# A hybrid diffusion backbone on one core: the MLP of both layers in two phases with seven products of the output kind, x kept in place

## The chip, the cores and the metric

One core of a Trainium2 chip runs the whole program in one launch. The metric is the device time in microseconds (us), the median over runs; the profile is one further execution, recorded by the hardware.

## The reference, cut to what matters

Two layers work on 1024 latent tokens of width 1024, and on 256 context tokens that only layer 0 carries on. Layer 0 mixes tokens by a Fourier part beside a state-space part, layer 1 by differential attention. Each layer then has the MLP that the change rewrites: hidden width 4096, squared ReLU, and a gated residual whose gate comes from the conditioning.

```python
def sq_relu_mlp(h, w1, w2):
    return jnp.square(jax.nn.relu(h @ w1)) @ w2
...
        x = x + g2 * sq_relu_mlp(modulate(rmsnorm(x, norm2_g[i]), sh2, sc2), mlp_w1[i], mlp_w2[i])
        if not last:
...
            ctx = ctx + cg2 * sq_relu_mlp(modulate(rmsnorm(ctx, norm2_g[i]), csh2, csc2), mlp_w1[i], mlp_w2[i])
```

## The kernel before, in words

Everything is kept feature by token: x of the latent tokens is a tile xL of 8 x 1024 columns on 128 partitions, x of the context is xC of 8 x 256. Latent tokens go in two blocks, t0 = 0 and t0 = 512, of 512 columns each; the context is a third block of 256. Every operand of a product is split into a high and a low part (`split`: a cast on ACT gives the high part, a subtraction on POOL or DVE the low one), and `mm3` (L341 to L343) makes three matmuls of a product.

The order of the work is written out by hand: a line of the program puts an instruction at the end of its engine's queue, and each engine takes its queue in order. Side work comes from generators in `bg`: `self.step()` at chosen places of the MLP emits the next small piece of the first one. These are the norm of the next stage (`norm`, L436: `norm_scale` with the matmuls L392 and L406, then `norm_apply` per 128 features) and `ada_dve` (L516 on), which makes the modulation of layer 1 on DVE out of 48 loads of 512 KB, with four or eight instructions of 256 columns for each load and column of the conditioning, and small matmuls L526. The class with `load`, `split`, `get` and `done` (L136 to L200) streams the weights: SP loads a raw tile into the ring R (three slots, shared with the ada loads), ACT and POOL split it into the ring W.

Layer 0 calls `mlp` (L1449 to L1506). It goes over pairs of 128 hidden features: the up products of both (banks 0 and 1, ReLU at L1465, square at L1466, split), then the down products of the pair (banks 2 to 5), which `stt` adds into x. Tile H (three buffers) holds the hidden features.

Layer 1 calls `mlp_w` (L1562 to L1738) in two phases. Phase 1 makes all hidden features; for each u (256 hidden features) DVE sums the four quarters (`results`), the seven operands are split and stored to DRAM h_w by SP (L1590). Phase 2 takes seven products for each c (512 hidden features, 0 to 6) and q (half of the output), with operands fetched by POOL's queue (L1652) into 24 tile slots and the weight sums of `down_weights` (L1517). The products rotate over 8 banks; all are summed in M apart from x, which was saved to DRAM and is fetched again; `together` (L1686) combines them on POOL, and the last four blocks of 128 hidden features are plain products. `put` writes the output (L2282).

Queues: PE takes matmuls in the order written; SP issues weight loads, ada loads and stores of h_w; POOL makes low parts and issues the fetches.

Of the kernel before, what the change touches and what calls it, by code (L numbers as in the profile page):

```python
# [201 lines left out]
class Kern:  # L202
# [988 lines left out]
    def first(self):  # L1191
# [216 lines left out]
        self.Y, self.Ypair = self.ring("Y", 3, 512), 1  # L1408
# [27 lines left out]
    def mlp_stream(self, layer):  # L1436
        I, add = self.I, self.ws.add
        up = lambda f: add(I["w1"][layer, f].rearrange("p a b -> p (a b)"))
        down = lambda f: add(I["w2"][layer, f].rearrange("p a b -> p (a b)"))
        for f in range(3):  # L1440
            up(f)
        for i in range(0, DFF // 128, 2):
            down(i)
            down(i + 1)
            for f in (i + 3, i + 4):
                if f < DFF // 128:
                    up(f)

    def mlp(self, layer, blocks, order, H, hook, before=None):  # L1449


        nf, nt = DFF // 128, sum(n for _, n in blocks)
        hb = [b.v(2, nt) for b in H]

        def up(f, w, bl, steps=()):
            o = hb[f % 3]
            for t0, n in bl:
                ps = self.bank(0, 1)[:, :n]
                hh, hl = self.hv(t0, n)
                for k in range(8):  # L1460
                    self.mm3(ps, w[:, 0, k], w[:, 1, k], hh[:, k], hl[:, k], k == 0, k == 7)
                    if k in steps and self.bg and self.bg[0][0][0] == "norm":
                        self.step()
                e = self.E.v(n)
                self.nc.scalar.activation(out=e, in_=ps, func=AF.Relu)  # L1465
                self.nc.scalar.activation(out=e, in_=e, func=AF.Square)  # L1466
                self.split(e, o[:, 0, t0:t0 + n], o[:, 1, t0:t0 + n], elo="p")
                self.step()

        def down(f, w, last):  # L1470
            for t0, n in blocks:
                for d in range(8):
                    ps = self.bank(2, 3, 4, 5)[:, :n]
                    for i in range(2):
                        a = hb[(f + i) % 3]
                        self.mm3(ps, w[i][:, 0, d], w[i][:, 1, d], a[:, 0, t0:t0 + n], a[:, 1, t0:t0 + n],
                                 i == 0, i == 1)
                    if last and (t0, n) == blocks[-1] and d == 7:
                        self.ws.pieces = 2
                        self.ws.done(1, elo="p")  # L1480
                        self.ws.done(1, elo="v")
                        self.ws.pieces = 1
                    x = self.xv(t0, n)[:, d]
                    g = self.mod_col(layer, 5, 0 if t0 < SEQ else 1)[:, d:d + 1]
                    self.stt(x, ps, g, x, ALU.mult, ALU.add)
                    if last:
                        hook(t0, n, d)
                    if last or d % 2:
                        self.step()

        w = [self.ws.get(8, 128) for _ in range(3)]
        for t0, n in order:
            if before:
                before(t0, n)
            for f in range(3):
                up(f, w[f], [(t0, n)], (0, 3, 5, 6, 7))
                if (t0, n) == order[-1]:
                    self.ws.done()
        for i in range(0, nf, 2):
            down(i, [self.ws.get(8, 128) for _ in range(2)], i + 2 >= nf)  # L1500
            if i + 2 < nf:
                self.ws.done(2)
            for f in (i + 3, i + 4):
                if f < nf:
                    up(f, self.ws.get(8, 128), blocks)
                    self.ws.done()  # L1506

# [7 lines left out]
    WINO = ("B11", "B21", "T2", "T3", "T1", "B22", "T4")  # L1515

    def down_weights(self, layer):  # L1517


        nc, I, raw = self.nc, self.I, {}  # L1520

        def load(u, i):
            raw[u, i] = r = self.R.v(1024)
            if u < 14:
                c, q = divmod(u, 2)
                o = r.rearrange("p (h f c) -> p h f c", h=2, f=2)
                for j in range(2):
                    src = I["w2"][layer, 4 * c + 2 * j + i].rearrange("p (h q d) e -> p h q (d e)", h=2, q=2)
                    nc.sync.dma_start(out=o[:, :, j], in_=src[:, :, q])
            elif u < 16:  # L1530
                o = r.rearrange("p (h f c) -> p h f c", h=2, f=4)
                for j in range(4):
                    nc.sync.dma_start(out=o[:, :, j], in_=I["w2"][layer, 28 + j][:, 2 * u - 28 + i::4])
# [5 lines left out]
        for u in range(16):  # L1539
            load(u + 1, 0)  # L1540
            A11, A21, A12, A22 = (raw[u, i][:, 512 * j:512 * j + 512] for i in range(2) for j in range(2))
            S1 = S2 = None
            for i in range(7 if u < 14 else 4):
                if i == 2 and u < 14:
                    S1, S2 = self.E.v(512), self.E.v(512)
                    self.tt(S1, A21, A22, ALU.add)
                    self.tt(S2, S1, A11, ALU.subtract)
                if i == 3 and u < 14:
                    self.tt(A21, A11, A21, ALU.subtract)
                if i == 5:  # L1550
                    self.tt(S2, A12, S2, ALU.subtract)
                src = (A11, A12, S2, A21, S1, S2, A22)[i] if u < 14 else (A11, A21, A12, A22)[i]
# [3 lines left out]
                self.split(src, w[:, 0].rearrange("p a b -> p (a b)"), w[:, 1].rearrange("p a b -> p (a b)"), elo="p")  # L1556
                n += 1
                if i == (5 if u < 14 else 1):
                    load(u + 1, 1)
                yield w  # L1560

    def mlp_w(self, layer, v0, oS, put):  # L1562


        nc, x8 = self.nc, self.xL.v(8, SEQ)
        fb, mb = self.buf("F", 2048), self.buf("M", 3072)
        dt = self.tc.dram_tile
        xd, hd = dt([128, 8, SEQ], F32R, name="x_w"), dt([16, 7, 128, 1024], F32R, name="h_w")
        fl = lambda a: a.bitcast(F32)
        for i in range(0, 8, 2):  # L1570
            nc.sync.dma_start(out=fl(xd)[:, i:i + 2], in_=x8[:, i:i + 2])

        X, L = fb.v(4, 512), self.xL.v(4, 512)
        turn = ([6, 7, 2, 3, 4, 5] * 17)[:98] + [2, 3, 6, 7, 6, 7, 6, 7]
        gen, Wq, count = self.down_weights(layer), [], [0, -1]

        def make(k=1):

            for _ in range(k):
                if count[0] < 106 and 2 * (count[0] // 2 - 3) + 1 <= count[1]:  # L1580
                    Wq.append(next(gen))
                    count[0] += 1


        def results(u, C):
            def keep(name, src, elo="p"):
                o = x8[:, turn.pop(0)].rearrange("p (a b) -> p a b", a=2)
                self.split(src, o[:, 0].bitcast(F32R), o[:, 1].bitcast(F32R), elo=elo)
                i = self.WINO.index(name) if name in self.WINO else 2
                nc.sync.dma_start(out=fl(hd)[u, i], in_=o.rearrange("p a b -> p (a b)"))  # L1590

            keep("B11", C["11"])
            yield
            if u > 13:
                for q in ("12", "21", "22"):
                    keep("B" + q, C[q])
                    yield
# [3 lines left out]
            keep("T1", T, "v")  # L1601
            yield
            keep("B22", C["22"])
            yield
            self.tt(T, C["22"], T, ALU.subtract)
            keep("T2", T)
            yield
            self.tt(C["12"], C["22"], C["12"], ALU.subtract)
            keep("T3", C["12"])
            yield  # L1610
            keep("B21", C["21"])
            yield
            self.tt(C["21"], C["21"], T, ALU.subtract)
            keep("T4", C["21"], "v")
            yield

        C, done = [{} for _ in range(16)], []

        def up(f, w, t0, beside):
            ps, (hh, hl), u = self.bank(0, 1), self.hv(t0, 512), f // 2  # L1620
# [3 lines left out]
            i = 2 * (f % 2) + t0 // 512  # L1624
            e = ((L if t0 else X)[:, f] if u < 2 else (X if u % 2 else L)[:, i])
            C[u][f"{1 + f % 2}{1 + t0 // 512}"] = e
            nc.scalar.activation(out=e, in_=ps, func=AF.Relu)
            nc.scalar.activation(out=e, in_=e, func=AF.Square)
            if f % 2 and t0:
                done.append(results(u, C[u]))  # L1630

        def norms(k):
            if k in (0, 3, 5, 6, 7) and self.bg and self.bg[0][0][0] == "norm":
                self.step()

# [6 lines left out]
        slots = [a[:, :, i, o:o + 512] for a, o in ((oS, 512), (v0, 0), (oS, 0)) for i in range(8)]  # L1642
        tiles, order = {}, [(c, j, p) for c in range(7) for j in range(7) for p in range(2)]
        order += [("x", d) for d in (0, 4, 1, 5, 2, 6, 3, 7)] + [(7, j, p) for p in range(2) for j in (0, 1, 2, 5)]

        def fetch(n):
            for _ in range(n):
                i = len(tiles)
                if i < len(order):
                    o, tiles[o] = order[i], slots[i % len(slots)]  # L1650
                    src = xd[:, o[1]] if len(o) == 2 else hd[2 * o[0] + o[2], o[1]]
                    nc.gpsimd.dma_start(out=tiles[o], in_=src.rearrange("p (a b) -> p a b", a=2))  # L1652

        w = [self.ws.get(8, 128) for _ in range(3)]
        for t0, n in LAT:
# [738 lines left out]
```

## Time and profile before

| what | value |
|---|---|
| runs | 2924.09, 2926.7, 2927.6 us, median 2926.7 |
| the profiled execution | 2926.48 us, its span 2924.7 us |
| mean granted clock of TensorE | 0.986 |
| PE busy | 2814.2 us, 96% of the span |
| DVE, POOL, ACT busy | 64%, 47%, 37% |
| DMA | 382.90 MB, 131 GB/s on average |

The span is what lies between the first and the last instruction; the 1.8 us around it do not change with the kernel's inside. Busy shares are means over very different stages. Layer 0's MLP runs from about 505 to 1420 us, layer 0's projection into layer 1 follows, and layer 1's MLP runs from about 2170 us to the end.

### The profile page before, as it was taken

To read this page: it belongs to the slowest core of one execution; us is meant where nothing else is said; L and a number is where in the kernel's file an instruction comes from. 1 tells how busy PE (TensorE), PEld (TensorE's weight loads), DVE (VectorE), ACT (ScalarE), POOL (GpSimd) and SP (SyncE) were. 2 spreads that over 40 slices of the span, in tenths; PEclk is the share of its full clock that TensorE was granted. 3 is DMA by queue.
4 is the path that set the end of the run, shared out by engine and by line. 5 is a ranking of instruction groups with operands and counts; after the bars stand their busy time and mean duration, and the time that the engine had idled before them with its cause. 6 is when DMAs were issued, how large, how long until landed. Compare 5 with 4: busy or idle time off the path is not lost.

```text
span 2924.7 us, 39807 instructions
## 1 busy us (share of the span) xinstructions
PE 2814.2 (96%) x15018; PEld 2352.2 (80%) x15018; DVE 1879.6 (64%) x3645; ACT 1077.5 (37%) x1915; POOL 1366.7 (47%) x1072
## 2 busy tenths in 40 slices
PE   5899899999999999999999999999999999999998
PEld 2666688788888888888778788999988888878887
DVE  7789867654553553232778857999976444337666
ACT  3342343322122222223334435666643544432220
POOL 5614223433232223223433425777733565568778
PEclk9999999999999999999999999999999999999999
DMA  7255540122222222101155642323224556598883
GB/s 296 88 186 165 177 133 24 44 87 73 80 87 79 80 72 74 42 29 44 44 161 159 165 127 86 98 75 108 71 87 137 201 214 232 194 309 274 252 259 123
DMA packets 240865, 382.90 MB, mean 131 GB/s; under 512 B 12960, under 2 KB 148640, under 8 KB 239648
## 3 DMA queue, kind: packets, MB, share of 16 engines
q1 hardware_dynamic: 199024, 293.31, 30.9%
q0 software_dynamic: 41648, 87.04, 9.9%
q8 instruction: 118, 1.93, 0.3%
q14 instruction: 75, 0.61, 0.1%
HBM read 270.69 MB, written 109.61 MB: 130 GB/s over the span
## 4 chain that ended last, share of the span: by engine, by line
PE 77%; DVE 12%; POOL 4%; ACT 3%; DMA 2%; issue 2%; SPq 0%; POOLq 0%; DVEq 0%; ACTq 0%
PE bank L341 20%; PE bank L342 20%; PE bank L343 20%; PE sc L1930 4%; PE pv L1970 4%; PE tb L1961 2%; DVE T L907 2%; DVE xh L911 2%; DVE E L296 2%; DVE hl L296 1%; POOL W L337 1%; PE sc L342 1%; PE sc L343 1%; PE sc L341 1%; POOL xL L324 1%
## 5 line engine op out<-in xcount | busy, mean ns | idle before, releaser
L337 POOL TENSOR_TENSOR W<-R,W 128x1024 fp32r<-128x1024 f32 (+1 forms) x170 | 340.7, 2012 | 572.3 <-issue 290.5
L296 DVE SCALAR_TENSOR_TENSOR xL<-bank,k,xL 128x512 f32<-128x512 f32 x296 | 217.7, 747 | 340.1 <-PE bank L343 339.7
L333 ACT CAST W<-R 128x1024 fp32r<-128x1024 f32 (+2 forms) x212 | 183.7, 884 | 506.7 <-PE bank L343 438.5
L341 PE MATMUL bank<-hl,W 128*128 128x512 f32 (+1 forms) x768 | 297.6, 387 | 8.1 <-ACT hl L433 3.8
L342 PE MATMUL bank<-hl,W 128*128 128x512 f32 (+1 forms) x768 | 295.3, 384 | 9.7 <-DVE hl L296 8.2
L343 PE MATMUL bank<-hl,W 128*128 128x512 f32 (+1 forms) x768 | 292.3, 381 | 1.0 <-DVE W L337 1.0
L341 PE MATMUL bank<-H,W 128*128 128x512 f32 (+1 forms) x768 | 274.6, 358 | 3.6 <-DVE xC L296 2.8
L342 PE MATMUL bank<-H,W 128*128 128x512 f32 (+1 forms) x768 | 271.8, 354 | 0.0
L343 PE MATMUL bank<-H,W 128*128 128x512 f32 (+1 forms) x768 | 271.8, 354 | 0.0
L337 POOL TENSOR_TENSOR H<-E,H 128x512 fp32r<-128x512 f32 (+1 forms) x96 | 107.9, 1124 | 231.6 <-ACT H L333 218.6
L343 PE MATMUL bank<-oS,W 128*128 128x512 f32 x536 | 208.8, 390 | 0.6 <-POOL W L337 0.6
L1935 DVE TENSOR_REDUCE S<-sc 128x1 f32<-128x1280 f32 x128 | 184.2, 1480 | 39.0 <-PE sc L1930 39.0
L342 PE MATMUL bank<-oS,W 128*128 128x512 f32 x536 | 209.0, 390 | 0.1
L341 PE MATMUL bank<-oS,W 128*128 128x512 f32 x536 | 208.9, 390 | 0.0
L341 PEld LDWEIGHTS bank<-hl,W 128*128 128x128 f32 x768 | 145.3, 189 | 58.4 <-issue 19.2
L342 PEld LDWEIGHTS bank<-hl,W 128*128 128x128 f32 x768 | 145.6, 190 | 42.3 <-DVE hl L296 14.9
L343 PE MATMUL bank<-hb,W 128*128 128x512 f32 x432 | 169.2, 392 | 3.6 <-POOL W L337 3.6
L341 PE MATMUL bank<-hb,W 128*128 128x512 f32 x432 | 169.3, 392 | 0.0
L342 PE MATMUL bank<-hb,W 128*128 128x512 f32 x432 | 168.8, 391 | 0.0
L343 PEld LDWEIGHTS bank<-hl,W 128*128 128x128 f32 x768 | 145.5, 190 | 28.6 <-DVE W L337 1.5
L1930 PE MATMUL sc<-K,W 128*128 128x512 f32 x720 | 167.8, 369 | 0.0
L341 PEld LDWEIGHTS bank<-H,W 128*128 128x128 f32 x768 | 145.2, 189 | 25.3 <-DVE xC L296 3.9
(441 smaller groups left out, 7079.9 us busy)
## 6 DMA issues: line engine op xcount, KB each, us to landing
h_w<-xL SPq DMA_DIRECT2D x106, 512.0 KB, 3.6
R<-in_w_dram SPq DMA_DIRECT2D x96, 512.0 KB, 3.7
oS<-h_w POOLq DMA_DIRECT2D x68, 512.0 KB, 7.7
R<-in_ada_w_dram SPq DMA_DIRECT2D x52, 512.0 KB, 3.6
hb<-h_w POOLq DMA_DIRECT2D x38, 512.0 KB, 7.1
W<-q_d POOLq DMA_DIRECT2D x15, 1024.0 KB, 5.4
R<-in_w_dram SPq DMA_DIRECT2D x56, 256.0 KB, 6.3
A<-in_ada_w_dram SPq DMA_DIRECT2D x24, 512.0 KB, 4.5
```

What stands on the lines that cost most here:

```text
L296: f(**kw)
L333: nc.scalar.copy(hi, src)
L337: e.tensor_tensor(out=lo, in0=src, in1=hi.bitcast(F32), op=ALU.subtract)
L341: mm(ps, lhsT=lh, rhs=rh, start=first, stop=False)
L342: mm(ps, lhsT=lh, rhs=rl, start=False, stop=False)
L343: mm(ps, lhsT=ll, rhs=rh, start=False, stop=last)
L907: v.tensor_tensor(out=b.raw(o, [[48, 2], [1, 32]]), in0=self.CAb.raw(64 * d, [[32, 2], [1, 32]]), in1=h.raw(prev[d], [[0, 2], [1, 32]]), o ...
L911: v.tensor_reduce(out=h.raw(cur[d], [[16, 2], [1, 16]]), in_=b.raw(o, [[48, 2], [1, 16], [16, 3]]), axis=AX.X, op=ALU.add)
L1930: nc.tensor.matmul(self.SC[i][:, c0:c0 + n], lhsT=Qf[:, e, q0:q0 + 128], rhs=K[:, i, c0:c0 + n], start=e == 0, stop=e == 1)
L1935: nc.vector.tensor_reduce(out=st[:, i, 1:2], in_=self.SC[i][:, 0:1280], axis=AX.X, op=ALU.max, negate=True)
L1961: nc.tensor.transpose(ps[:, 128 * j:128 * j + 128], it["P"][0][:, 128 * (c0 + j):128 * (c0 + j) + 128], self.ident)
L1970: nc.tensor.matmul(self.PV[:, 0:128], lhsT=it["wT"][:, kt], rhs=heads[h]["v"][:, kt], start=kt == 8, stop=kt == 3)
```

## The change

One function `mlp` serves both layers and has the two phases; `mlp_w` and the DRAM copy of x are gone.

- Of the seven products of a (c, q), three (j = 1, 5, 6) feed one quarter of the output only. Their results go from the bank straight into x (`to_x`). The four shared ones (j = 0, 2, 3, 4) are summed in M, 16 half tiles, and `together` has four additions on POOL and four `to_x` in place of seven additions and four.
- Products use banks 0 to 5 (8 before in layer 1). In layer 0 the context has plain down products in banks 6 and 7; `down_weights` splits an eighth half (A21) for them.
- Layer 0 has 16 tile slots in the buffers of the normalized input (h0, h1) and four for the context in hc, which are free once the up products have read them; layer 1 has 22. The splits of `results` go through 3 places (layer 0) or 4 (layer 1; 6 before).
- `up` steps the side work by two pieces a block. `self.flush()` empties it ahead of hidden block 30.
- The last products of layer 0 go in two passes over the features: blocks 0 and context first, then block 512, with three pieces of side work each.
- Layer 0's down products for the latent tokens were 1536 matmuls of 512 columns; over 28 of the 32 hidden blocks seven of eight are left. PE's queue has 11324 rows where it had 11492, 168 fewer, all of them of 512 columns.

```diff
-    def mlp(self, layer, blocks, order, H, hook, before=None):
...
-    def mlp_w(self, layer, v0, oS, put):
...
+    def mlp(self, layer, order, slots, sc, ready, hook, before):
+        nc, blocks = self.nc, sorted(order)
+        ctx = len(order) == 3
...
+        turn = ([10, 12, 14] if ctx else [8, 10, 12, 14]) * 50
...
             if ctx:
+                keep(7, place(8 + u % 2))
+                yield
+            keep(0, C["11"])
...
         def up(f, w, t0, n, beside):
...
             nc.scalar.activation(out=e, in_=ps, func=AF.Relu)
             nc.scalar.activation(out=e, in_=e, func=AF.Square)
-            if f % 2 and t0:
+            left[f] -= 1
+            if left[2 * u] + left[2 * u + 1] == 0:
                 done.append(results(u, C[u]))
+            self.step(2)
...
+        for f in range(3, 30):
             w = self.ws.get(8, 128)
+            for t0, n in blocks:
+                up(f, w, t0, n, keeps)
             self.ws.done()
+        self.flush()
+        next(gen)
+        fetch_free(None)
+        w = [self.ws.get(8, 128) for _ in range(2)]
+        free = [None]
+        for t0, n in blocks:
+            for f in (30, 31):
+                make(count[0] < 2)
+                up(f, w[f - 30], t0, n, keeps)
+            free.append(t0)
+            if t0 != blocks[-1][0]:
+                fetch_free(*free)
+        self.ws.done(2)
         make(6)
+        fetch_ctx(0)
+        fetch_free(*free)
...
+                        if j in (1, 5, 6):
+                            to_x(ps, dh if j == 6 else dl, 512 if j == 5 else 0)
                         else:
+                            m = place(M[q][j, e])
+                            if c:
+                                self.tt(m, ps, m, ALU.add)
+                            else:
+                                self.vcopy(m, ps)
+                    if ctx and j in (0, 1, 6):
+                        for e in range(2):
+                            context(w, e, int(j > 0), int(j == 6))
+                    used()
...
+        if ctx:
+            ready(0)
+            for i, d in enumerate(self.LAST):
+                last(Wq.pop(0), d, 512, 512)
+                used()
+                hook(512, 512, d, i)
+                self.step(3)
+                if i % 2:
+                    ready(i)
...
-        self.mlp(0, ALL, MIX, [H0, H1, H2], hook, before=lambda t0, n: self.flush_norm(t0))
+        slots = [(0, h0[:, :, i]) for i in range(6)] + [(512, h1[:, :, i]) for i in range(4)] + \
+                [(0, h0[:, :, i]) for i in (6, 7)] + [(512, h1[:, :, i]) for i in range(4, 8)]
...
+        self.mlp(0, MIX, slots, sc, ready, hook, before)
```

Four places where the order of instructions matters. First SP in layer 0's up phase, over one pair of hidden blocks (L1539 stores a split operand, L544 is an ada load, L149 a weight load). Before, the same loads had no stores between them:

```order
L544 DMA R_50_5350<-in_ada_w_dram 128x4x256
L149 DMA R_51_5390<-in_w_dram 128x1024
L544 DMA R_52_5439<-in_ada_w_dram 128x4x256
L544 DMA R_53_5509<-in_ada_w_dram 128x4x256
L544 DMA R_54_5578<-in_ada_w_dram 128x4x256
```

```order
L149 DMA R_90_7127<-in_w_dram 128x1024
L1539 DMA h_w_4555<-M_4839 128x1024
L1539 DMA h_w_4555<-M_4554 128x1024
L1539 DMA h_w_4555<-M_4839 128x1024
L544 DMA R_91_7167<-in_ada_w_dram 128x4x256
L1539 DMA h_w_4555<-M_4839 128x1024
```

Three stores now stand ahead of the ada load of R_91. On DVE, in the same pair, the instructions on that load (Y from R) stand ahead of sums of hidden features (E and M):

```order
L296 TENSOR_TENSOR E_184_7156<-M_4554 128x512
L337 TENSOR_TENSOR M_4839<-E_184_7156,M_4839 128x512
L296 TENSOR_SCALAR Y_16_7166<-R_91_7167,k_110 128x256
L296 SCALAR_TENSOR_TENSOR Y_16_7166<-R_91_7167,k_110,Y_16_7166 128x256
L296 TENSOR_TENSOR E_184_7156<-M_4554,E_184_7156 128x512
L296 TENSOR_TENSOR M_4554<-M_4554 128x512
```

The sum in E_184 is an operand that ACT casts ahead of the next ReLU. Next POOL at the switch of layer 0 between the phases (hl are the buffers of the two latent blocks, hc that of the context; L1604 is a fetch):

```order
L1604 DMA hl_3675<-h_w_4555 128x2x512 x6
L1604 DMA hl_3679<-h_w_4555 128x2x512 x4
L1604 DMA hl_3675<-h_w_4555 128x2x512 x2
L1604 DMA hl_3679<-h_w_4555 128x2x512 x4
L337 TENSOR_TENSOR W_57_8255<-E_189_8059,W_57_8255 128x512
L337 TENSOR_TENSOR W_57_8255<-E_190_8060,W_57_8255 128x512
L337 TENSOR_TENSOR W_58_8261<-E_188_8058,W_58_8261 128x512
L337 TENSOR_TENSOR W_58_8261<-E_189_8059,W_58_8261 128x512
L1604 DMA hc_3828<-h_w_4555 128x2x512 x4
```

The context's fetches stand last, behind sixteen others and four splits. Last PE: at `self.flush()` ahead of hidden block 30 (hc is the context's up product of block 29), and in layer 0's projection into layer 1:

```order
L343 MATMUL bank_1_61<-hc_3828,W_53_7688 128x256
L526 MATMUL bank_7_67<-k_94,Y_21_7899 128x1 x2
L526 MATMUL bank_7_67<-k_94,Y_22_7998 128x1 x2
L526 MATMUL bank_7_67<-k_94,Y_23_8014 128x1 x2
L526 MATMUL bank_7_67<-k_94,Y_24_8030 128x1 x2
L341 MATMUL bank_0_60<-hl_3675,W_54_7782 128x512
```

```order
L343 MATMUL bank_2_62<-W_122_11473,hl_3675 128x512
L392 MATMUL bank_6_66<-k_110,Y_30_11640 128x1 x4
L406 MATMUL bank_7_67<-E_272_11694,k_94 128x512
L341 MATMUL bank_3_63<-W_120_11364,hl_3679 128x512
```

The small matmuls of four chunks of `ada_dve` come one behind the other, with no product between them; in the projection the two matmuls of the norm of block 512 (L392, L406) are neighbours, where before 18 matmuls stood between them.

## Rows read from the trace of the kernel before

**Rows 1.** The page: busy time by engine, and the chain's shares by engine.

```profile
PE 2814.2 (96%) x15018; PEld 2352.2 (80%) x15018; DVE 1879.6 (64%) x3645; ACT 1077.5 (37%) x1915; POOL 1366.7 (47%) x1072
PE 77%; DVE 12%; POOL 4%; ACT 3%; DMA 2%; issue 2%; SPq 0%; POOLq 0%; DVEq 0%; ACTq 0%
```

**Rows 2.** Windows: stretch, its length, busy time (count) of each engine, clock, DMA share, GB/s.

```profile
850.00:1000.00 150.00, 150.00 (x798) 129.78 (x798) 75.37 (x124) 35.33 (x56) 43.24 (x26) 1.00 0.26 81
2614.00:2619.00 5.00, 1.38 (x5) 0.84 (x4) 1.29 (x2) 0.00 (x0) 4.70 (x6) 0.79 1.38 385
```

**Rows 3.** Timeline of the end: start, time, engine, line, operation, [idle before <-releaser].

```profile
2911.72 0.39 PE L342 MATMUL bank<-hb,W 128*128 128x512 f32 x1
...
2915.35 0.39 PE L343 MATMUL bank<-oS,W 128*128 128x512 f32 x1
2915.39 1.71 POOL L324 TENSOR_TENSOR M<-F,M 128x512 f32<-128x512 f32 x1
...
2919.55 2.05 DVE L296 SCALAR_TENSOR_TENSOR M<-bank,k,M 128x512 f32<-128x512 f32 x3
```

**Rows 4.** Timeline of layer 1's switch between the phases.

```profile
2615.16 0.71 POOL L1652 DMA_DIRECT2D oS<-h_w  x1 [0.28 <-DMA hb<-h_w]
...
2617.12 2.49 POOL L337 TENSOR_TENSOR W<-R,W 128x512 fp32r<-128x512 f32 x2
...
2618.43 0.80 PE L343 MATMUL bank<-hb,W 128*128 128x512 f32 x1 [3.62 <-POOL W L337]
```

**Rows 5.** Timeline of PE at the start of layer 0's MLP, and at its end.

```profile
516.59 0.39 PE L341 MATMUL bank<-hc,W 128*128 128x256 f32 x1 [2.05 <-ACT E L1465]
...
1416.09 0.39 PE L341 MATMUL bank<-H,W 128*128 128x256 f32 x1 [1.33 <-DVE xC L296]
1416.31 0.28 PE L342 MATMUL bank<-H,W 128*128 128x256 f32 x1
1416.43 0.29 PE L343 MATMUL bank<-H,W 128*128 128x256 f32 x1
...
1419.57 0.76 PE L341 MATMUL bank<-W,hl 128*128 128x512 f32 x1 [2.50 <-DVE xC L296]
1420.13 0.63 PE L342 MATMUL bank<-W,hl 128*128 128x512 f32 x1
...
1425.25 0.59 PE L342 MATMUL bank<-W,hl 128*128 128x512 f32 x1
```

**Rows 6.** Timeline of the norm in layer 0's projection.

```profile
1432.05 0.94 PE L392 MATMUL bank<-k,Y 128*128 128x1 f32 x8
1438.14 0.59 ACT L409 COPY Y<-bank 128x512 f32<-128x512 f32 x1 [3.01 <-PE bank L406]
1452.58 0.75 DVE L296 SCALAR_TENSOR_TENSOR hl<-E,k,hl 128x512 fp32r<-128x512 f32 x1 [0.19 <-ACT hl L433]
```

**Rows 7.** Groups by line and shape, 560 to 1370 us: count | busy, mean ns | idle before.

```profile
L341 PE MATMUL bank<-H,W 128*128 128x512 f32 x470 | 184.4, 392 | 0.7 <-DVE xL L296 0.7
L296 DVE SCALAR_TENSOR_TENSOR xL<-bank,k,xL 128x512 f32<-128x512 f32 x236 | 173.6, 748 | 295.7 <-PE bank L343 295.6
L337 POOL TENSOR_TENSOR W<-R,W 128x1024 fp32r<-128x1024 f32 x56 | 135.5, 2431 | 321.9 <-issue 267.0 <-ACT W L333 54.9
L296 DVE SCALAR_TENSOR_TENSOR Y<-R,k,Y 128x256 f32<-128x256 f32 x218 | 123.9, 598 | 34.6 <-DMA R<-in_ada_w_dram 31.7
L337 POOL TENSOR_TENSOR H<-E,H 128x512 fp32r<-128x512 f32 x56 | 72.8, 1301 | 180.4 <-ACT H L333 180.4
```

**Rows 8.** Timeline: an ada load in layer 0's MLP, and DVE's first instructions on it.

```profile
1013.51 0.38 SPq L544 DMA_DIRECT2D R<-in_ada_w_dram  x1
1017.14 1.00 DVE L296 SCALAR_TENSOR_TENSOR Y<-R,k,Y 128x256 f32<-128x256 f32 x2 [1.72 <-DMA R<-in_ada_w_dram]
```

**Rows 9.** Timeline of POOL in the norm: one operation beside little of DVE, one beside much.

```profile
1441.27 1.30 POOL L324 TENSOR_TENSOR E<-xL,Y 128x512 f32<-128x512 f32 x1
1443.73 1.74 POOL L324 TENSOR_TENSOR E<-xL,Y 128x512 f32<-128x512 f32 x1
```

More of the change, by code (lines that the diff above doesn't have):

```diff
@@ L1433, in hv @@
         return [a[:, :, t0 - b:t0 - b + n] for a in self.hx[b]]
+    WINO = ("B11", "B21", "T2", "T3", "T1", "B22", "T4")
+    LAST = (0, 1, 4, 5, 2, 3, 6, 7)
     def mlp_stream(self, layer):
[L1437 to L1447, printed above, removed]
@@ L1449, in mlp @@
-    def mlp(self, layer, blocks, order, H, hook, before=None):
[L1452 to L1506, printed above, removed]
@@ L1515, with down_weights @@
-    WINO = ("B11", "B21", "T2", "T3", "T1", "B22", "T4")
-    def down_weights(self, layer):
+        for f in range(32):
+            self.ws.add(self.I["w1"][layer, f].rearrange("p a b -> p (a b)"))
+    def down_weights(self, layer, plain, passes):
         nc, I, raw = self.nc, self.I, {}
+        end = 14 + 2 * passes
         def load(u, i):
-            raw[u, i] = r = self.R.v(1024)
+            if u < end:
+                raw[u, i] = r = self.R.v(1024)
             if u < 14:
@@ L1646, in fetch, with get @@
+        def get(o, v):
+            tiles[o] = v
+            nc.gpsimd.dma_start(out=v, in_=hd[2 * o[0] + o[2], o[1]].rearrange("p (a b) -> p a b", a=2))
+        n_slots, fetched = len(slots), [0]
         def fetch(n):
             for _ in range(n):
[L1648 to L1652, printed above, removed]
+                i = fetched[0]
+                if i < len(tasks):
+                    get(tasks[i], slots[i % n_slots][1])
+                    fetched[0] += 1
@@ L1654, in mlp_w, with fetch_free, fetch_ctx @@
+        def fetch_free(*free):
+            while fetched[0] < n_slots and slots[fetched[0]][0] in free:
+                fetch(1)
+        def fetch_ctx(c):
+            if ctx and c < 8:
+                for p in range(2):
+                    get((c, 7, p), sc[2 * (c % 2) + p])
         w = [self.ws.get(8, 128) for _ in range(3)]
-        for t0, n in LAT:
-            self.flush_norm(t0)
+        for t0, n in order:
+            before(t0, n)
+            if (t0, n) == order[-1]:
+                mem.append(self.buf("M", 2048, side="R"))
@@ L1657, in mlp_w @@
             for f in range(3):
[L1658 to L1659 removed]
+                up(f, w[f], t0, n, norms)
+                if (t0, n) == order[-1]:
                     self.ws.done()
[L1661 removed]
+        for f in range(3, 30):
             w = self.ws.get(8, 128)
[L1663 to L1673 removed]
```

299 lines of the change are left out of this document (173 added, 126 removed).

## Prediction

> **What bounds the kernel now.** I read the page first: PE is busy 96% of the span and makes 77% of the chain that ended last [rows 1]. The kernel is a stream of matmuls with a few holes, and a change is worth what it takes out of the stream and the holes it closes, less the holes it opens. The windows show the stream: from 850 to 1000 us PE is busy the whole 150 us at full clock [rows 2]. Next comes the timeline at each hole that lies in code the change touches: the end [rows 3], layer 1's switch from up to down products [rows 4], start and end of layer 0's MLP [rows 5]. DVE, ACT and POOL have room on average [rows 1], but each takes its queue in order, so a hole comes from one late item at the head of a queue.
>
> Two prices. A 512-column matmul: the one at 2911.72 and the one at 2915.35 are 16 steps apart [rows 3], 0.2269 us each (the 0.39 us in a row is the latency of one, not the pace). And what a hole costs beyond its length: after the gap of 2.50 us before 1419.57, the 12 steps from 1420.13 to 1425.25 take 0.427 us each [rows 5], TensorE then being at the lower of its levels, so 12 x 0.20 = 2.4 us more. After the gap of 1.33 us at 1416.09 the 256-column matmuls at once start 0.12 us apart again. I charge 2.4 us to a hole above 2 us and nothing to one below 1.4.
>
> **The change, term by term**, against the profiled execution's own 2926.48 us, which lies 0.2 us under the median of the runs.
>
> 1. *Fewer matmuls.* Layer 0 loses 168 matmuls of 512 columns: 168 x 0.2269 = **-38.1**. Layer 1 has seven products already and keeps its count.
>
> 2. *The end.* The last matmul starts at 2915.35; POOL still adds, DVE's last three additions run to 2921.60, the span ends 3.1 us later at 2924.7 [rows 3], 9.35 us after that start. Now the last product goes from its bank to x in one `stt` (0.75 us [rows 7]) and out: 0.39 + 0.75 + 3.1 = 4.2. So **-5.1**.
>
> 3. *Layer 1's switch.* POOL issues sixteen fetches in a row, waits for a landing before it may issue the last, and only then makes low parts of weights [rows 4]. In the 5 us from 2614 PE makes five matmuls, 1.1 us of work [rows 2], so 3.9 are lost, and the clock's 2.4 behind. Now the last eight fetches stand behind the six splits of `make(6)`, and six tiles have a buffer of their own: **-6.3**.
>
> 4. *Layer 0's small holes.* Its start has a gap of 2.05 us behind a ReLU on ACT [rows 5]; the down products waited 0.7 us for x over 470 groups [rows 7]. The norms are stepped earlier, and the fused loop is gone: **-2.8** (0, if the ReLU is late again, to -5.2 with the clock).
>
> 5. *Layer 0 into layer 1.* The context's `stt` held the banks at the end: the two later gaps of [rows 5], smaller ones and the slow matmuls, 8.8 us, with 2 us in the norm behind 10.8 in all. The last pass over block 512 takes the first part away. But that block's norm now comes last, and its two matmuls are neighbours on PE, where 18 products lay between. The chain of the norm now: small matmuls at 1432.05, y at 1438.73 (6.7 us), the last feature at 1453.33 (14.6 more) [rows 6]. With 2.2 us for the last squares ahead, and 24 x 0.227 = 5.4 us of products that go on beside the features, PE lacks 2.2 + 6.7 + 14.6 - 5.4 = 18. The context's norm is as close and has only 6 products between, 5.5 us, and two holes lose the clock: 28.3 against 10.8, **+18** (5, if side work fills it, to 25).
>
> 6. *`flush()` ahead of block 30.* The sums of four chunks of ada work stand on PE with no product between; before, they lay beside products. Six loads remain. One lands 3.6 us after its issue [rows 8], and four instructions of 0.50 us on it make 2.0; the three raw slots overlap the landings, so DVE sets the pace: 6 x 2.0 = 12, with the clock **+14** (4, if only two loads are left, to 18).
>
> 7. *The context's first tiles* are fetched last. At 385 GB/s [rows 2] a tile of 512 KB takes 1.36 us. Ten fetches that wait for block 512's up products can start 5.4 us before the last up product ends; with 2.5 us for the first to arrive, the tenth lands at -5.4 + 2.5 + 13.6 = 10.7 after that end. POOL, held by the limit on open fetches as in [rows 4] and by four low parts of 1.3 us, issues the context's fetches late, and they land at 13 to 13.5. PE wants them after 12 products, at 2.7: 10.6 and the clock, **+13** (5 to 16).
>
> 8. *Layer 0's up phase, the largest term.* A pair of hidden blocks has 2 x (5.44 + 5.44 + 2.72) = 27.2 us of products. The ReLU that frees a bank stands on ACT behind casts of sums; the sums stand on DVE behind additions of an ada load; the load stands on SP behind three stores, and these wait for low parts on POOL. From the pair's last matmul: POOL ends the low part of the weights (2.43 [rows 7]) at 4.3 and two operands (1.25 each; 1.30 in [rows 7]) at 6.8, SP issues the load at 7.65, it lands at 12.3 (3.6 by [rows 8], and one more behind three stores), two ada additions to 13.3, sums to 14.55, a cast and the ReLU on ACT (0.6 each, as the copy in [rows 6]) to 15.75. PE wants the bank at 13.6, or at 14.6 where small matmuls and their waits stand between: 1.2 to 2.2 us late, 1.75 on average. 13 pairs have ada work; in the first five, each load feeds both columns of the conditioning, 1 us more. 8 x 1.75 + 5 x 2.75 = 28. About four holes exceed 2 us by enough to lose the clock, 9: **+37** (0 to 28 + 13 x 2.4 = 59).
>
> The rest has no price. Layer 0 now stores and fetches 122 operands, 128 MB more over some 900 us, 140 GB/s where the DMA can move 385 [rows 2]. POOL gets 137 more instructions, about 180 us, hidden where it is idle (busy 47% [rows 1]); without that cover the weights come late, as in [rows 4]. Six banks in place of eight cost nothing: four banks lost 0.7 us in 470 groups [rows 7].
>
> Sum: -38.1 - 5.1 - 6.3 - 2.8 + 18 + 14 + 13 + 37 = +29.7; 2926.5 + 29.7 = **2956**.
>
> For POOL in term 8 the trace has two values of one operation: 1.30 us beside little of DVE, 1.74 beside a DVE addition [rows 9]. I used the low end, as DVE waits for the load just then. Three of POOL's items at 0.44 us more bring the load 1.3 us later in 13 pairs, 17 us: 2973. The Trainium skill ("SBUF — State Buffer", section "SBUF: two separate sides") says that a DVE instruction with two operands in SBUF and a GpSimd instruction that reads there take a shared port in turn, each for its whole length. By that rule the dearer value holds wherever both are at work; [rows 9] agree in kind.
>
> **Rivals.**
>
> - *The load comes in time* (the other side). Term 8 hangs on one late arrival at the end of a chain of ten links. If the load lands 2.2 us sooner, 10.1 us after the pair's last matmul, no ReLU is late, and the term is 0: 2926.5 - 7.3 = 2919, faster; with the context's tiles in time too, 2906. For it: stores need not delay a load, and small errors of each link add up. Against it: DVE already waits 31.7 us for ada loads [rows 7], with no stores ahead of them.
> - *Half of it.* Landing 1.7 us sooner leaves 8 to 14 us of term 8: 2927 to 2933, about no change.
> - *Cold all along, or POOL at the dear price.* All 13 pairs lose the clock (59 for 37), or POOL's items take 1.74: 2973 to 2978. For it: the hole over 2 us followed in [rows 5] lost the clock, and [rows 9]. Against it: few pairs go far beyond 2 us.
> - *The change does not do what it says.* The order shows the 168 matmuls gone; I give this nothing.
>
> **How the numbers follow.** 0.2% (5.9 us) is about what a measurement of this kernel can tell from no change. The load in time 0.20; half of it 0.12; the forecast 0.46, from 2933 to 2968; dear 0.22. Faster by over 0.2% is the first: 0.20. Same is most of the second: 0.10. Slower is the rest, 0.70. The range goes from 2905 (load and tiles in time) to 2985 (dear, with terms 5 to 7 near their tops); what is left out is terms 5 to 7 near their low ends together with the first rival, some 2885, and larger losses.
>
> **What would show it.** In the changed kernel's trace: 168 fewer 512-column matmuls; no hole at layer 1's switch; the span's end 4 us behind the last matmul. In layer 0: a hole of 10 to 13 us ahead of block 30, with the sums of ada work as releaser; one of about 10 us in the first down products, released by a fetch into hc; one of 5 us or more between the two small matmuls of block 512's norm in the projection; and in the up phase a wait of 1 to 3 us on a ReLU in each of 13 pairs, ACT waiting there for DVE, and DVE for an ada load. The prediction is wrong if the pairs show no such wait (the first rival), or if the down phase, which I cost at its matmuls alone, waits for weights or tiles.

## The result, and the profile after

| what | before | after |
|---|---|---|
| median | 2925.39 us | 3014.82 us (3011.04 to 3016.74) |
| ratio | | 1.0304, interval 1.0286 to 1.0322 |
| the profiled execution, its span | 2926.48, 2924.7 | 3013.48, 3011.7 |
| mean granted clock | 0.986 | 0.971 |

The change made the kernel slower by 3.0%, 89 us; forecast was 2956 us, 30 slower, in a range that ended at 2985. The side was right, the size was not.

The page after, first the busy line and the shares of the chain by engine, which answer to [rows 1], then two groups of its fifth part (the first is the first matmul of a product with an operand in the latent blocks' buffers; the second the additions of ada work on DVE):

```profile
PE 2815.6 (93%) x14850; PEld 2342.4 (78%) x14850; DVE 1967.2 (65%) x3694; ACT 1131.9 (38%) x2036; POOL 1559.2 (52%) x1282
...
PE 68%; DVE 12%; DMA 7%; issue 5%; ACT 4%; POOL 3%; SPq 0%; DVEq 0%; POOLq 0%; ACTq 0%
...
L341 PE MATMUL bank<-hl,W 128*128 128x512 f32 (+1 forms) x1224 | 490.7, 401 | 70.2 <-ACT M L1581 61.5
...
L296 DVE SCALAR_TENSOR_TENSOR Y<-R,k,Y 128x256 f32<-128x256 f32 x224 | 152.4, 713 | 102.2 <-DMA R<-in_ada_w_dram 99.0
```

PE has the 168 matmuls less (15018 to 14850) and is busy as long as before, since a matmul at the lower clock takes longer (rows of 0.63 us behind the holes, of 0.39 elsewhere). In 61.5 us it stands idle and is released by L1581, the ReLU on ACT, almost all of it in layer 0's up phase. DVE stood idle for ada loads 31.7 us in layer 0's MLP before [rows 7]; now it is 99.0. That group leaves out the first instruction on the first load of each chunk, a `TENSOR_SCALAR`; ahead of it DVE was idle for 66.4 us in layer 0's MLP before and is for 107.0 now.

The stretches, as in [rows 2] (length, then busy time and count of PE, PEld, DVE, ACT, POOL, then clock, DMA share, GB/s): most of layer 0's up phase, the flush, the context's tiles, the way into the projection, a piece of layer 1's up phase, and layer 1's switch.

```profile
600.00:1000.00 400.00, 349.97 (x1771) 298.79 (x1770) 180.24 (x277) 146.51 (x257) 155.22 (x99) 0.95 0.56 197
1013.00:1025.00 12.00, 3.52 (x20) 3.26 (x18) 9.78 (x24) 0.80 (x2) 0.00 (x0) 0.61 0.80 244
1055.00:1068.00 13.00, 3.60 (x15) 2.51 (x13) 2.94 (x3) 3.38 (x7) 10.20 (x10) 0.69 1.24 345
1478.00:1545.00 67.00, 41.78 (x156) 30.19 (x155) 42.44 (x79) 23.25 (x46) 24.23 (x20) 0.80 0.15 48
2400.00:2500.00 100.00, 100.00 (x438) 81.94 (x437) 41.51 (x27) 49.34 (x78) 57.64 (x33) 1.00 0.55 202
2690.00:2730.00 40.00, 37.72 (x156) 29.97 (x156) 24.65 (x31) 10.65 (x20) 32.65 (x33) 0.96 1.03 323
```

Up to the first score matmul of layer 1's attention the changed kernel is 86.3 us behind (1849.6 for 1763.4). From the last matmul into the banks of the scores (sc) to the last matmul of all it needs 674.15 us for 668.56, and the end behind that is 5.0 shorter: 86.3 + 5.6 - 5.0 = 86.9 of the 87.0 us between the profiled executions. So the loss lies in layer 0 and its projection into layer 1.

One pair of layer 0's up phase in the changed kernel's timeline, from the last small matmuls of a pair to the late product of the next (L1539 stores a split operand, L544 is an ada load):

```profile
911.86 0.50 PE L526 MATMUL bank<-k,Y 128*128 128x1 f32 x4
...
913.53 4.49 DVE L296 SCALAR_TENSOR_TENSOR Y<-R,k,Y 128x256 f32<-128x256 f32 x3
...
913.91 2.40 POOL L337 TENSOR_TENSOR W<-R,W 128x1024 fp32r<-128x1024 f32 x1 [7.41 <-ACT W L333]
...
917.95 1.77 DVE L296 TENSOR_TENSOR E<-M 128x512 f32<-128x512 f32 x1
...
918.47 2.97 SPq L1539 DMA_DIRECT2D h_w<-M  x3
...
919.75 0.62 ACT L333 CAST M<-E 128x512 fp32r<-128x512 f32 x1 [4.88 <-DVE E L296]
...
920.41 0.69 DVE L337 TENSOR_TENSOR M<-E,M 128x512 fp32r<-128x512 f32 x1 [0.69 <-ACT M L333]
...
921.50 0.90 SPq L544 DMA_DIRECT2D R<-in_ada_w_dram  x1
...
927.55 1.00 DVE L296 SCALAR_TENSOR_TENSOR Y<-R,k,Y 128x256 f32<-128x256 f32 x2 [6.39 <-DMA R<-in_ada_w_dram]
...
929.24 0.62 ACT L333 CAST M<-E 128x512 fp32r<-128x512 f32 x1 [5.04 <-DVE E L296]
...
930.32 0.59 ACT L1581 ACTIVATE M<-bank 128x512 f32<-128x512 f32 x1
...
930.97 0.80 PE L341 MATMUL bank<-hl,W 128*128 128x512 f32 x1 [4.70 <-ACT M L1581]
```

This is the chain of term 8, link by link, and each link is there: the third store needs an operand that DVE makes (920.41 to 921.10), the ada load stands behind it (921.50), DVE waits 6.39 us for the load, two additions and a sum later ACT has a cast, another, and then the ReLU, and PE waits for that. Such holes stand ahead of every second hidden block, thirteen with ada work in all, 2.7 to 6.5 us long and 54.9 us together.

### The profile page after: what moved, and what is told of

It reads as the page before. It is cut to its first block, busy times and chain, and to the rows that moved or that the text cites. A ratio compares the mean times of both kernels' runs of the same rounds, so it can differ in the third digit from the quotient of the medians.

```text
span 3011.7 us, 40545 instructions
## 1 busy us (share of the span) xinstructions
PE 2815.6 (93%) x14850; PEld 2342.4 (78%) x14850; DVE 1967.2 (65%) x3694; ACT 1131.9 (38%) x2036; POOL 1559.2 (52%) x1282
## 4 chain that ended last, share of the span: by engine, by line
PE 68%; DVE 12%; DMA 7%; issue 5%; ACT 4%; POOL 3%; SPq 0%; DVEq 0%; POOLq 0%; ACTq 0%
PE bank L341 17%; PE bank L343 16%; PE bank L342 16%; DMA R<-in_ada_w_dram 4%; PE sc L1957 4%; PE pv L1997 4%; DVE Y L296 4%; PE tb L1988 2%; DVE E L296 2%; DVE S L296 1%; PE sc L342 1%; PE sc L343 1%; PE sc L341 1%; POOL M L337 1%; DVE hl L296 1%
## 5 line engine op out<-in xcount | busy, mean ns | idle before, releaser
L337 POOL TENSOR_TENSOR W<-R,W 128x512 fp32r<-128x512 f32 (+1 forms) x196 | 341.1, 1750 | 509.9 <-ACT W L333 501.9
L341 PE MATMUL bank<-hl,W 128*128 128x512 f32 (+1 forms) x1224 | 490.7, 401 | 70.2 <-ACT M L1581 61.5
L342 PE MATMUL bank<-hl,W 128*128 128x512 f32 (+1 forms) x1224 | 482.4, 394 | 5.5 <-DVE hl L296 5.5
L343 PE MATMUL bank<-hl,W 128*128 128x512 f32 (+1 forms) x1224 | 479.9, 392 | 1.0 <-DVE W L337 1.0
L341 PE MATMUL bank<-hb,W 128*128 128x512 f32 x968 | 381.8, 394 | 3.2 <-ACT W L333 1.7
L343 PE MATMUL bank<-hb,W 128*128 128x512 f32 x968 | 379.7, 392 | 1.3 <-POOL W L337 1.3
L342 PE MATMUL bank<-hb,W 128*128 128x512 f32 x968 | 377.4, 390 | 0.0
L341 PEld LDWEIGHTS bank<-hl,W 128*128 128x128 f32 x1224 | 238.3, 195 | 141.8 <-ACT M L1581 64.4
L333 ACT CAST W<-R 128x512 fp32r<-128x512 f32 (+2 forms) x237 | 184.7, 798 | 303.2 <-PE bank L343 157.3
L342 PEld LDWEIGHTS bank<-hl,W 128*128 128x128 f32 x1224 | 238.3, 195 | 52.9 <-DVE hl L296 9.8
L343 PEld LDWEIGHTS bank<-hl,W 128*128 128x128 f32 x1224 | 237.2, 194 | 50.2 <-DVE W L337 1.4
L296 DVE SCALAR_TENSOR_TENSOR Y<-R,k,Y 128x256 f32<-128x256 f32 x224 | 152.4, 713 | 102.2 <-DMA R<-in_ada_w_dram 99.0
L343 PEld LDWEIGHTS bank<-hb,W 128*128 128x128 f32 x968 | 182.0, 188 | 43.5 <-POOL W L337 2.1
L341 PEld LDWEIGHTS bank<-hb,W 128*128 128x128 f32 x968 | 182.2, 188 | 43.0 <-ACT W L333 2.5
L342 PEld LDWEIGHTS bank<-hb,W 128*128 128x128 f32 x968 | 182.2, 188 | 40.0 <-issue 0.2
L296 DVE TENSOR_TENSOR M<-bank,M 128x512 f32<-128x512 f32 x192 | 131.2, 689 | 105.5 <-PE bank L343 105.4
L337 POOL TENSOR_TENSOR W<-E,W 128x512 fp32r<-128x512 f32 x112 | 144.9, 1312 | 98.6 <-ACT W L333 98.4
L1581 ACT ACTIVATE M<-bank 128x512 f32<-128x512 f32 (+1 forms) x160 | 88.4, 553 | 264.4 <-PE bank L343 264.3
L324 POOL TENSOR_TENSOR R<-R,S 128x896 f32<-128x896 f32 x64 | 107.3, 1677 | 111.2 <-DVE S L296 94.2
```

Of the source, the lines that this page charges most:

```text
L296: f(**kw)
L324: self.nc.gpsimd.tensor_tensor(out=o, in0=a, in1=b, op=op)
L333: nc.scalar.copy(hi, src)
L337: e.tensor_tensor(out=lo, in0=src, in1=hi.bitcast(F32), op=ALU.subtract)
L341: mm(ps, lhsT=lh, rhs=rh, start=first, stop=False)
L342: mm(ps, lhsT=lh, rhs=rl, start=False, stop=False)
```

## The experiments

Times are medians; the kernel before, run beside them, was at 2924 to 2927 us.

**1. The sums first.** While sums of hidden features are pending, no ada work is emitted:

```diff
-            self.step(2)
+            if not self.bg or self.bg[0][0] != "ada":
+                self.step(2)
+            elif not done:
+                self.step(4)
```

> The change with one thing moved: while sums of hidden features are pending, no piece of the ada work is emitted; it comes in the other three of the six blocks of a pair, four pieces a block where there were two. Theory A (the ReLU is late because the sums stand on DVE behind additions that wait for an ada load): the holes of 2.7 to 6.5 us in front of every second hidden block go, 64 us of gaps and 15 to 20 us of low clock with them; 2930 to 2945 us. Theory B (the chain of casts, low parts and stores through three places is itself too long): ReLU still late by 2 us or more in each pair; above 2985 us. The holes at block 30, at the context's tiles and at the projection stay in both.

Measured: 3045.04 us, ratio 1.0414 (1.0396 to 1.0431). Neither theory had that. The ReLU is late no more, but PE waits elsewhere. The groups of PE from 540 to 1010 us in this run (count | busy, mean ns | idle before):

```profile
L341 PE MATMUL bank<-hl,W 128*128 128x512 f32 x411 | 167.7, 408 | 0.3 <-ACT M L1581 0.2
...
L526 PE MATMUL bank<-k,Y 128*128 128x1 f32 x104 | 20.8, 314 | 71.6 <-DVE Y L296 71.6
```

The same rows of the changed kernel:

```profile
L341 PE MATMUL bank<-hl,W 128*128 128x512 f32 x440 | 183.4, 417 | 55.8 <-ACT M L1581 55.8
...
L526 PE MATMUL bank<-k,Y 128*128 128x1 f32 x112 | 13.7, 235 | 0.3 <-DVE Y L296 0.3
```

The hole has moved to the small matmuls that sum a chunk of ada work. The timeline of this run shows what they wait for:

```profile
885.77 0.43 SPq L544 DMA_DIRECT2D R<-in_ada_w_dram  x1
...
890.43 0.35 DVE L296 TENSOR_SCALAR Y<-R,k 128x256 f32<-128x256 f32 x1 [5.05 <-DMA R<-in_ada_w_dram]
...
892.38 6.02 SPq L544 DMA_DIRECT2D R<-in_ada_w_dram  x2
...
895.95 2.05 DVE L296 SCALAR_TENSOR_TENSOR Y<-R,k,Y 128x256 f32<-128x256 f32 x4 [3.53 <-DMA R<-in_ada_w_dram]
...
898.05 1.01 PE L526 MATMUL bank<-k,Y 128*128 128x1 f32 x4 [5.01 <-DVE Y L296]
```

A load is issued only when DVE is done with the one before (892.38): of the three raw slots the ada work has one, and its three loads of a pair go one behind the other, close to 6 us each. So theory A was right about the ReLU, and wrong that nothing else would be late; its time lies 100 us above the forecast.

**2. The context's tiles first** at the switch (the first lines; the fetches of block 512 then come in two parts around the splits):

```diff
-        free = [None]
-        for t0, n in blocks:
+        free, ends = [None], blocks[2:] + blocks[:2]
+        for t0, n in ends:
...
+            if t0 == SEQ:
+                fetch_ctx(0)
```

> The change with another order at layer 0's switch: hidden blocks 30 and 31 go context first, so its four tiles are fetched first, then block 0's six, then four of block 512, the weight splits, and the rest. If the hole of 9.2 us in front of the context's first down product comes from the place of its fetches in POOL's queue, it goes with its slow clock: 3002 to 3005 us. Rival: the tiles are bound by DMA traffic, so that another tile is late instead: 3012 to 3017 us.

Measured: 3008.56 us, ratio 1.0289 (1.0274 to 1.0305), 6 us under the change where 10 to 13 were expected, and with an interval that overlaps that of the change (1.0286 to 1.0322); so the trace has to show it. The hole of the changed kernel,

```profile
1066.75 0.58 PE L341 MATMUL bank<-hc,W 128*128 128x256 f32 x1 [9.16 <-DMA hc<-h_w]
```

is gone; one of 2.34 us stands there instead, in which PE waits for DVE to empty a bank of the context.

**3. Other passes** over the last products of layer 0:

```diff
-            for t0, n in (blocks[0], blocks[2 if ctx else 1]):
+            for t0, n in blocks[:1 if ctx else 2]:
...
-                last(Wq.pop(0), d, 512, 512)
+                w = Wq.pop(0)
+                for t0, n in blocks[1:]:
+                    last(w, d, t0, n)
```

> The change with the last products of layer 0 split otherwise: the first pass has block 0 alone, the second has block 512 and the context. Theory: the 13 us hole in front of the projection comes from DVE, where evictions stand behind pieces of two norms squeezed into 22 us of products; with the norm of block 0 spread over 33 us of products, and the norms of block 512 and the context behind, as in the kernel before, the 28 us of holes around the projection shrink to about 10: 2993 to 3000 us. Rival: the norm of block 512 is late anyway and the holes only move: 3010 to 3017 us.

Measured: 2993.31 us, ratio 1.0233 (1.0218 to 1.0248), 21.5 us under the change, as the theory had it. The 12.91 us hole is 1.74 us now, and the norm's holes behind are gone; a new one of 3.95 us for weights stands in the first pass, which has less PE work to hide their splits (this reason is argued, not tried).

**4. The three edits together**, with five pieces of ada work a block in place of four.

> The three edits together, and five pieces of ada work a block in place of four, so that none is left to flush ahead of block 30 (about 14 us). If each hole has its own cause, the gains add: 70 to 85 + 11 + 18 + 13 us from 3015, so 2885 to 2905 us, faster than the kernel before. If they share a cause (one engine simply has too much work), the sum falls short by 20 us or more: above 2920 us.

Measured: 3008.1 us, ratio 1.0283 (1.0268 to 1.0299). The time is on the side of the shared cause, but the trace is not: the two gains of experiments 2 and 3 are there, and the loss of experiment 1 with them. From experiment 1's 3045.0 us it is 36.9 down, 27.8 for those two gains, which leaves some 9 for the flush ahead of block 30.

**5. No ada work in the up phase at all** (all of it in the flush ahead of hidden block 30):

```diff
-            self.step(2)
+            if not self.bg or self.bg[0][0] != "ada":
+                self.step(2)
```

> A probe, meant to be slow: no piece of the ada work is emitted in the up phase, all 48 loads come at the flush ahead of hidden block 30. Theory A (ada work in DVE's and SP's queue makes the ReLU late): the up phase has no hole above 1 us between its third and its fifteenth pair, and the flush takes 48 x 4 to 5 us; about 3120 to 3180 us in all. Theory B (three places for the splits, POOL's low parts or the stores alone make it late): holes of 2 us or more in each pair are left.

Measured in a single run: 3027.82 us, some 90 under the forecast. Windows of the up phase and of the flush, and PE's first group from 540 to 1010 us:

```profile
600.00:900.00 300.00, 299.63 (x1561) 257.75 (x1560) 74.69 (x66) 138.55 (x239) 144.12 (x86) 1.00 0.50 186
920.00:1037.00 117.00, 30.61 (x129) 28.55 (x130) 104.51 (x275) 0.83 (x2) 2.06 (x7) 0.51 0.67 209
```

```profile
L341 PE MATMUL bank<-hl,W 128*128 128x512 f32 x440 | 171.9, 391 | 0.5 <-ACT M L1581 0.5
```

Without ada work the up phase runs with no hole, and three places, POOL's low parts and the stores do well: theory A in its mechanism. The flush of all 48 loads takes 117 us, 2.4 a load, half of what I expected; with nothing else in the queues the loads overlap and DVE sets the pace. That gives a price for ada work in the changed kernel: the last product ahead of the flush starts at 1013.2 us there and at 918.8 here, 94.4 us later.

**6. Up weights one block ahead**, where it was two, so that the ada work has two raw slots (sums first as in experiment 1):

```diff
-        self.load()
+        if self.nl < self.ns + self.depth:
+            self.load()
...
+                self.ws.depth = 1
```

> The sums first as in e1_sums_first, and up weights are loaded one block ahead where it was two while the ada work runs. In e1_sums_first three ada loads of a pair went one after the other through one of the three raw slots (issued 885.8, 892.4, 898.0 us), and PE waited 5 to 8 us for their sums in each pair; the other two slots held raw up weights. Theory C (the raw slots are the limit): with a second slot for ada loads the holes at the small matmuls go, 100 us under e1_sums_first: 2930 to 2960. Rival (load and four additions, 6 us each, are too much for the half of the pair that is left, whatever the slots): 2990 or more.

Measured: 3025.82 us, ratio 1.0341 (1.0323 to 1.0358): 19 under experiment 1, far from the 100 of theory C and in the range of the rival. The holes at the small matmuls are still 2.5 to 6.5 us. Whether the rival's reason holds (the work itself is too much) is tried in experiment 8.

**7. All of it with one block ahead.**

> e5_one_ahead with the context's tiles first, the other passes, and five pieces of ada work a block (none left to flush). The two edits gave 6 and 22 us alone. Theory C: under 2915 us, so faster than the kernel before; rival of e5_one_ahead: 2960 or more.

Measured: 2959.75 us, ratio 1.0117 (1.01 to 1.0134). That is at the edge of the rival's 2960, in the same way.

**8. The small matmuls a load later**, so that PE asks for the chunk before last:

```diff
...
-                if late:
-                    sums(late[1], late[2])
+                if late and kh:
+                    sums(late[1], late[2])
+                    summed = late
...
```

> e5_one_ahead with the small matmuls that sum a chunk of ada work emitted one load later (at the end of the next chunk, where they stood in its middle). In e5_one_ahead PE waits 2.5 to 6.5 us at them in each of 13 pairs, 57 us of gaps and about 25 of low clock, for additions on the load just before. Theory D (PE waits only because the small matmuls are asked for a load too soon; DVE and the queue do the three loads of a pair in time): the holes go, 2935 to 2955 us. Rival (the loads fall behind over the pairs): 2975 or more, or a longer hole at the flush.

Measured: 2954.42 us, ratio 1.0101 (1.0086 to 1.0116), 71 us under experiment 6. PE's groups from 540 to 1010 us (the edits moved L341 to L342, L526 to L527):

```profile
L342 PE MATMUL bank<-hl,W 128*128 128x512 f32 x480 | 190.4, 397 | 2.5 <-ACT M L1583 2.2
...
L527 PE MATMUL bank<-k,Y 128*128 128x1 f32 x128 | 18.6, 258 | 19.5 <-DVE k L297 19.5
```

Theory D: DVE and the queues do the work in time once nobody on PE asks too soon, which also answers the rival of experiment 6. Of the 19.5 us that are left, 12.9 lie in the flush.

**9. All of it with late sums**, and **10. the same with the offset of experiment 11.**

> e6_all_one_ahead with the same late sums. Theory D: the 46 us of gaps and 20 of low clock at the small matmuls go: 2890 to 2905 us, faster than the kernel before by about 1%. Rival: 2930 or more.

> e10_all_late_sums with the 1088 bytes of e7_offset. If the offset is what it was there (443 matmuls in 100 us again), 3 to 5 us under e10_all_late_sums.

Measured: 2912.34 us, ratio 0.9958 (0.9941 to 0.9974), and 2905.98 us, ratio 0.9938 (0.9923 to 0.9953): both beat the kernel before, by 0.4% and 0.6%, little but clear of their intervals. The first lies above its 2890 to 2905: holes of 2.3 to 5.7 us are left at the start of block 512's up products, in two pairs, at the context's first products and in the first of the last passes. The second is 6.4 us under the first where 3 to 5 were expected, with intervals that overlap, and has its 443 matmuls from 2400 to 2500 us. Its page:

```profile
PE 2783.5 (96%) x14850; PEld 2325.1 (80%) x14850; DVE 1964.2 (68%) x3694; ACT 1132.3 (39%) x2036; POOL 1558.6 (54%) x1282
```

**11. An offset of 1088 bytes** ahead of the normalized input in layer 1:

```diff
+        gap = b("gap", 272, side="R")
         hb0 = b("hb0", 2 * 8 * 512, True, "R")
```

> The change with one thing moved: 1088 unused bytes a partition ahead of the normalized input of layer 1's MLP (hb0), which shifts where it lies. In layer 1 the change makes 438 matmuls in 100 us of its up phase at full clock where the kernel before makes 443, in a pattern that repeats with each pair of blocks, and I can't see a wait there. If it is where the operand lies, the pace goes back to 443, 4 to 6 us in all: 3008 to 3012. If not, 3014 to 3016.

Measured: 3012.26 us, ratio 1.0296 (1.0281 to 1.0312), 2.6 under the change, within the spread of the runs. But the window of the trace is plain:

```profile
2400.00:2500.00 100.00, 100.00 (x443) 82.83 (x442) 40.43 (x28) 48.90 (x78) 54.33 (x32) 1.00 0.57 205
```

443 matmuls where the changed kernel makes 438, and from the last matmul into sc to the last matmul 669.65 us for 674.15: 4.5 us. The same bytes also move a part of M that layer 1's MLP allocates behind hb0 on that side, so this shows that a place matters, not that it is hb0's.

## Why the prediction was wrong, step by step

*Terms 1 and 2* came as written: 168 matmuls fewer, and at the end

```profile
3007.38 0.39 PE L343 MATMUL bank<-hb,W 128*128 128x512 f32 x1
...
3007.80 0.75 DVE L296 SCALAR_TENSOR_TENSOR xL<-bank,k,xL 128x512 f32<-128x512 f32 x1 [2.02 <-PE bank L343]
```

one addition and the way out, 4.3 us from the last matmul's start to the span's end where it was 9.35: -5.0 for -5.1.

*Term 3* failed. The hole of 3.62 us [rows 4] is gone, but three of 1.47, 0.96 and 1.33 us, behind the ReLU and behind weights on ACT and POOL, with a slow clock around the last two, cost nearly as much: 37.72 us busy of 40 at a clock of 0.96. I had taken the fetches' new place for the whole cause; weights and tiles still meet on POOL. With the pace that the offset cost (4.5), layer 1 up to its last matmul lost 5.6 where I had -6.3.

*Term 4* gave nothing: the gap of 2.05 us went, and one of 1.06 with it, but one of 5.68 came in front of block 512's up products, for a ReLU again: 2.6 more, where I had -2.8.

*Terms 6 and 7* held: 11.9 us from the flush's first small matmul to the next product (14 forecast), and 9.46 us of holes for the context's tiles with some slow matmuls behind (13 forecast).

*Term 5* had the loss, and one place more than I saw. I had PE waiting inside the projection, at the norm of block 512; it does, 2.7, 3.1 and 4.1 us. The largest hole comes before:

```profile
1484.99 0.74 DVE L296 SCALAR_TENSOR_TENSOR xL<-bank,k,xL 128x512 f32<-128x512 f32 x1
1485.85 4.47 DVE L296 TENSOR_TENSOR Y<-Y,E 128x256 f32<-128x256 f32 x5
1490.78 0.42 DVE L296 TENSOR_TENSOR Y<-Y,E 128x256 f32<-128x256 f32 x1 [0.46 <-DVE Y L296]
1491.12 0.74 DVE L296 SCALAR_TENSOR_TENSOR xL<-bank,k,xL 128x512 f32<-128x512 f32 x1
...
1492.01 0.76 PE L341 MATMUL bank<-W,hl 128*128 128x512 f32 x1 [12.91 <-DVE xL L296]
```

The evictions of the last products (`stt` from a bank into xL) stood on DVE behind pieces of two norms, so a bank came free late; experiment 3 took the hole away. From 1478 to 1545 PE makes 156 matmuls, 12 of them of one column; 144 x 0.227 is 32.7 us of 67, and two gaps of 1.1 and 1.4 stood before. That is 36.8 us lost for 28.3 forecast; against the 10.8 of before, +26 for +18.

*Term 8* is the step that failed. Its mechanism was right, its size was not: 94.4 us between a phase with and one without ada work, less the 14 us or so of small matmuls that the kernel before had too (an estimate from its trace, where a group of four puts the next product off by about 0.5 us and one of eight by 0.9), is about 80 for 37. The thirteen holes make 54.9 us of it where I had 28, and what is left, about 25, is mostly low clock, where I had 9. "From the pair's last matmul" I had the load issued at 7.65 us, landed at 12.3, the ReLU done at 15.75. In the pair shown, from 912.0 us, it was issued at 9.5, landed at 15.5, and the ReLU ended at 18.9. Two links carry that.

Over the thirteen pairs the last load is issued 4.7 us ahead of the hole (3.3 to 6.1), where the sum had 5.95 or 6.95 (13.6 or 14.6 less 7.65), and DVE starts on it 5.3 us after its issue (4.2 to 7.0), where I had 4.65. These two cover the 2.1 us by which the mean hole of 4.2 is longer than forecast. In the pair shown, DVE was not waiting "just then", as I had argued for the cheap value of POOL's price: it was at the load before, and three of its additions took 4.49 us beside POOL's low parts of the weights and of an operand; three such take 1.52 us with POOL idle, and the sum behind took 1.77 for 0.68 (928.48 us). The three one by one, POOL's operands, and three with POOL idle:

```profile
913.53 0.48 DVE L296 SCALAR_TENSOR_TENSOR Y<-R,k,Y 128x256 f32<-128x256 f32 x1
914.05 2.54 DVE L296 SCALAR_TENSOR_TENSOR Y<-R,k,Y 128x256 f32<-128x256 f32 x1
...
916.26 2.91 POOL L337 TENSOR_TENSOR M<-M,M 128x512 fp32r<-128x512 f32 x2
...
916.62 1.40 DVE L296 SCALAR_TENSOR_TENSOR Y<-R,k,Y 128x256 f32<-128x256 f32 x1
...
941.11 1.52 DVE L296 SCALAR_TENSOR_TENSOR Y<-R,k,Y 128x256 f32<-128x256 f32 x3
```

So I looked for the price of their meeting on POOL's side, and it stood mostly on DVE's (POOL's two operands took 2.91 us, where one alone takes 1.28 at 924.28). And the load was 6.0 us on its way with four other 512 KB transfers ahead of it, where I had 4.65. The hole was 4.7 us and not 1.2 to 2.2, and none of the thirteen is under 2.7 us, so nearly every pair lost the clock too: 0.95 over the phase.

The Trainium skill ("SBUF — State Buffer", section "SBUF: two separate sides") says that whichever of the two starts first has the shared port for its whole length and the other waits; by it DVE's additions would stretch as seen here. The rows agree: the low part of the weights (913.91, 2.40 us) ends at 916.31 and the addition that began beside it at 916.59, the next low part at 917.74 and the next addition at 918.02. Over the up phase and the flush 178 of the 224 additions take 0.48 us, and each of the other 46 ends 0.3 us behind an instruction of POOL; these waits add 52 us to DVE's work, where they added 26 before. How much of term 8's miss this made, apart from the slow landing, was not tried by itself.

Closing the sum for layer 0 by what was measured: -38.1 + 80 + 12 + 11 + 26 + 2.6 = +93.5, for 86.3. Of the 7 us between them the changed kernel's profiled execution gained 3.3 ahead of the MLP, in work that the change leaves alone (the first up product starts at 499.4 us, before at 502.6); the 4 or so that remain I have not taken apart.

*The rivals.* "Cold all along, or POOL at the dear price" was the nearest, 2973 to 2978; it had both mechanisms and priced each as if the other did not matter. Both added up give 2995, still 20 short: the chain that I priced link by link ran later than either allowed.

## What to carry to other kernels

Work that was free beside one loop is not free beside another: 48 loads took slots, queue places and DVE time between plain products, and fewer places between sums that PE waited for. When a change packs side work into half the time, list for each queue what will stand behind its waits, and ask of each fix what is late next: here the ReLU, then the raw slot, then a small matmul that asked one load too soon; the three together gave the time back. The later small matmul without the other two was not tried. A link that looks late by 1 us will be late by more where two engines slow each other, so price a chain from rows in which its neighbours run too.

## What the runs showed of the hardware that I had not expected

Two kernels with the same matmuls of 512 columns at full clock, in layer 1's up phase from 2400 to 2500 us, went at 0.2291 us a step and, with 1088 unused bytes in front of hb0, at 0.2267, with no wait in the trace: 1.1%. Experiments 9 and 10 repeat it (0.2292 and 0.2267). In the slower one the steps follow one fixed pattern that repeats every 48 matmuls: 34 of them are uneven, up to 0.237 us, and 14 keep 0.2267. Which tile's place matters (hb0's, or that of the part of M behind it), and what it shares with another operand, was not tried.

DVE's additions were not slowed evenly beside POOL: 0.48 us alone, and 1.4 to 2.7 us when they began beside an instruction of POOL, so that they ended 0.3 us behind it. POOL lost little: its low part of the weights kept its 2.40 us, two operands took 2.91 for twice 1.28.
